# A row-sum kernel whose first block is loaded by four strided DMAs instead of one

## The chip, the cores and the metric

The kernel runs on one core of a Trainium2 chip. The metric is device time in microseconds, from one execution; the median of three runs of the kernel before is 160.64 us (160.61 to 160.81). A profiled execution of the same program gives the time inside: its span runs from the first to the last instruction that the profiler records, and the rest of the execution lies around that span.

## The reference

The input x has the shape 32 x 512 x 1024 in float32, that is 16384 rows of 1024 numbers, 67.1 MB. Each row is summed and the sum multiplied by 0.5; the output is 32 x 512 in float32.

```
def reference(x, multiplier):
    return (np.sum(x, axis=-1) * multiplier).astype(np.float32)
```

## The kernel before

The 16384 rows are spread over the 128 partitions of the on-chip memory (SBUF), 128 rows for each. They are worked through in eight blocks of B = 16 rows for each partition, so that a block is 128 partitions x 16 rows x 4 KB = 8 MB, 64 KB for each partition. In the first seven blocks, a partition's 112 rows lie one after another in the input (`x_rows`, line 43), so that the 64 KB of one partition and block are contiguous there, and neighbouring partitions lie 448 KB apart. The last block (`x_last`, line 44) is the last 2048 rows of the input.

All loads are issued by SyncE, through the helper `load` (lines 73 to 79): one DMA from the input into a buffer, a semaphore of its own that the DMA raises by 16 when all of it has landed, and, from the fourth block on, a wait until VectorE has finished with the buffer (`bufs` = 3 buffers, line 51, used in turn). The DMA queue of SyncE is served by 16 DMA engines that each take a share of a transfer's partitions.

The first three loads wait for nothing. The function `start_loads_at_entry` (lines 184 to 208) moves such leading loads into the program's entry block, ahead of SyncE's part of the barrier with which all engines begin; it takes every load up to the first that has a wait.

In the loop over blocks (lines 104 to 134), VectorE waits for the block's landing (line 114), sums all rows of it in one instruction (`reduce_sum`, lines 115 to 120) and scales the sums into `res` (line 122). In the seventh block VectorE takes eight of the rows and ScalarE the other eight, with one activation each that scales and sums (`act_row`, line 82).

The last block (lines 136 to 174) comes in five pieces of falling size, 10 rows, 4 rows, 1 row with a part of the last row, and the two other parts of that row, so that little is left to sum when the last piece lands. VectorE sums with `dve_sum` (line 92), ScalarE with `act_row`. The outputs of the first seven blocks are stored early (line 151), those of the last one at the end (line 177), and SyncE waits for both.

The change touches the first pass of the loop, where b is 0: its load and the value that VectorE waits for.

Of the kernel before, what the change touches and what calls it, by code (L numbers as in the profile page):

```python
# [9 lines left out]
def kernel(  # L10
# [13 lines left out]
    nc = tc.nc  # L24
# [4 lines left out]
    P = nc.NUM_PARTITIONS  # L29
# [9 lines left out]
    B = 16  # L39
# [3 lines left out]
    x_rows = x_flat[0 : P * own, :].rearrange("(p c) d -> p c d", p=P)  # L43
# [7 lines left out]
    bufs = 3  # L51
# [4 lines left out]
    at = 368  # L56
    end = sbuf("end", P, at + D - cuts[1])

    def sem(name):
        return nc.alloc_semaphore(name=name)  # L60
# [5 lines left out]
    def marks(i, engine):  # L66

        s = dve_done if engine == "dve" else act_done
        i.then_inc(s, 1)
        counts[engine] += 1  # L70
        return counts[engine]

    def load(name, dst, src, free=None):
        landed = sem(name)
        i = nc.sync.dma_start(out=dst, in_=src)  # L75
        if free is not None:
            i.wait_op(dve_done, free, "sem-ge")
        i.then_inc(landed, 16)
        return landed

    def act_row(t, r, col):
        return nc.scalar.activation(  # L82
            out=t[:, r, :],
            in_=t[:, r, :],
            func=mybir.ActivationFunctionType.Copy,
            scale=mul,
            accum_out=res[:, col : col + 1],
        )
# [14 lines left out]
    freed = []  # L103
    for b in range(n_blocks - 1):
        c0 = b * B
        t = buf[b % bufs]
        landed = load(
            f"landed{b}",
            t,
            x_rows[:, c0 : c0 + B, :],  # L110
            freed[b - bufs] if b >= bufs else None,
        )
        h = B if b < n_blocks - 2 else B // 2
        nc.vector.wait_ge(landed, 16)
        done = marks(
            nc.vector.reduce_sum(  # L116
                out=sums[:, c0 : c0 + h], in_=t[:, 0:h, :], axis=mybir.AxisListType.X
            ),
            "dve",
        )  # L120
        freed.append(done)
        scaled = nc.vector.tensor_single_scalar(  # L122
            out=res[:, c0 : c0 + h],
            in_=sums[:, c0 : c0 + h],
            scalar=mul,
            op=mybir.AluOpType.mult,
        )
        scaled.wait_op(dve_done, done, "sem-ge")
        early_dve = marks(scaled, "dve")
        if h < B:  # L130
            nc.scalar.wait_ge(landed, 16)
            for r in range(h, B):
                i = act_row(t, r, c0 + r)
            early_act = marks(i, "act")

    c0 = (n_blocks - 1) * B
    t = buf[(n_blocks - 1) % bufs]
# [4 lines left out]
    landed = [  # L142
        load(f"landed_p{k}", flat[:, lo:hi], flat_last[:, lo:hi])
        for k, (lo, hi) in enumerate(zip(bounds[:-1], bounds[1:]))
    ]
# [11 lines left out]
    for k, (lo, hi) in enumerate(((0, 10), (10, 14), (14, 15))):  # L157
        on = [r for r in range(lo, hi) if r in on_act]
        nc.scalar.wait_ge(landed[k], 16)
        for r in on:  # L160
            i = act_row(t, r, c0 + r)
        late_act = marks(i, "act") if k == len(landed) - 1 else None
        on = [r for r in range(lo, hi) if r not in on_act]
        nc.vector.wait_ge(landed[k], 16)
        for r in on:
            dve_sum(t[:, r, :], res[:, c0 + r : c0 + r + 1], mul)
# [79 lines left out]
```

## Time and profile before

| quantity | value |
|---|---|
| median of 3 runs | 160.64 us (160.61 to 160.81) |
| time of the profiled execution | 160.62 us |
| its span | 159.3 us |
| VectorE busy | 119.9 us, 75% |
| ScalarE busy | 16.3 us, 10% |
| share of the 16 DMA engines that the queue filled | 98.1% |
| read from HBM, mean rate over the span | 67.11 MB, 422 GB/s |
| first reduction of VectorE starts | 21.76 us |
| from a load's issue to its landing, median of 7 | 40.8 us |

In the profile, DVE is VectorE, ACT is ScalarE, POOL is GpSimd and SP is SyncE; SPq is SyncE's sequencer, which issues the DMAs. L116 is line 116 of the kernel. In a timeline, each row has a start and a length in microseconds, engine, line, operation, what is written and read, and how often; square brackets show for how long the engine stood idle before it, and what ended that. In a table of windows, each row has the window and its length, the busy time of the engines with the number of their instructions, the granted clock of TensorE (1.00 here, where it does no work), the share of the DMA engines' time and the rate in GB/s; a DMA packet counts, with all its time and bytes, in the window where it starts. In a chain of waits, each row has a start, a length and what the time went to.

### The profile page before, as it was taken

How to read it: one execution, taken by the hardware profiler on the slowest of the kernel's cores; microseconds unless marked ns; L12 is line 12 of the kernel's file. 1: busy time of each engine (PE TensorE's matmuls, PEld its weight loads, DVE VectorE, ACT ScalarE, POOL GpSimd, SP SyncE). 2: the span in 40 equal slices, each digit the busy share in tenths (PEclk: the TensorE clock that was granted, in tenths of full speed). 3: DMA queues.
4: the chain of work that ended last, by engine and by line, in shares of the span. 5: the costliest groups of instructions: out<-in, count | busy, mean ns of one | idle time of the engine just before them, and what ended most of it. 6: DMA issues, size and time to landing. Idle time of an engine off the chain costs nothing.

```text
span 159.3 us, 123 instructions
## 1 busy us (share of the span) xinstructions
DVE 119.9 (75%) x38; ACT 16.3 (10%) x29; POOL 0.2 (0%) x4
## 2 busy tenths in 40 slices
DVE  0000059998699968999599995999959999598376
ACT  3000000000000000000000000000000000397384
POOL 0000000000000000000000000000000000000000
DMA  7996996997998989969969969969989699799994
GB/s 263 527 527 263 527 527 263 527 477 313 527 411 378 527 346 444 527 280 510 527 263 527 527 263 527 494 296 527 428 362 527 296 494 527 329 432 391 415 404 151
DMA packets 2016, 67.18 MB, mean 422 GB/s; under 512 B 480, under 2 KB 736, under 8 KB 864
## 3 DMA queue, kind: packets, MB, share of 16 engines
q1 hardware_dynamic: 2016, 67.18, 98.1%
HBM read 67.11 MB, written 0.07 MB: 422 GB/s over the span
## 4 chain that ended last, share of the span: by engine, by line
DMA 75%; DVE 24%; SPq 0%; issue 0%
DMA xb<-in_x_dram 75%; DVE sums L116 22%; DVE xb L92 1%; DVE end L92 0%; SPq L75 0%; DVE res L122 0%; DVE res L92 0%
## 5 line engine op out<-in xcount | busy, mean ns | idle before, releaser
L116 DVE TENSOR_REDUCE sums<-xb 128x16 f32<-128x16384 f32 (+1 forms) x7 | 112.0, 16001 | 33.3 <-DMA xb<-in_x_dram 33.3
L82 ACT ACTIVATE xb<-xb 128x1024 f32<-128x1024 f32 x14 | 14.6, 1044 | 139.1 <-DMA xb<-in_x_dram 139.1
L92 DVE CUSTOM_DVE_ANT_0 xb<-xb 128x512 f32<-128x512 f32 (+1 forms) x10 | 5.9, 654 | 4.4 <-DMA xb<-in_x_dram 4.4
L82 ACT ACTIVATION_READ_ACCUMULATOR xb<-xb 128x1 f32 x14 | 2.6, 186 | 0.0
L82 ACT ACT_TABLE_LOAD x1 | 1.3, 1283 | 2.4 <-PEq L26 2.4
L122 DVE TENSOR_SCALAR res<-sums 128x16 f32<-128x16 f32 (+1 forms) x7 | 1.2, 174 | 0.2
L92 DVE DVE_READ_ACCUMULATOR2_ANT res<- 128x1 f32 x10 | 0.8, 82 | 0.0
L92 DVE CUSTOM_DVE_ANT_0 end<-end 128x176 f32<-128x176 f32 (+1 forms) x2 | 0.7, 326 | 0.0
L92 DVE DVE_READ_ACCUMULATOR2_ANT end<- 128x1 f32 x2 | 0.2, 84 | 0.0
L227 POOL MEMSET const-bfloat16-1.0<- 128x1 bf16 x1 | 0.1, 101 | 0.0
L227 POOL MEMSET const-uint8-127<- 128x1 uint8 x1 | 0.1, 101 | 0.0
L227 POOL MEMSET const-float32-0.0<- 128x1 f32 x1 | 0.1, 98 | 0.2 <-issue 0.2
L227 POOL MEMSET const-float32-1.0<- 128x1 f32 x1 | 0.1, 98 | 0.0
## 6 DMA issues: line engine op xcount, KB each, us to landing
xb<-in_x_dram SPq DMA_DIRECT2D x1, 5120.0 KB, 33.6
xb<-in_x_dram SPq DMA_DIRECT2D x1, 2048.0 KB, 38.1
xb<-in_x_dram SPq DMA_DIRECT2D x1, 704.0 KB, 39.3
end<-in_x_dram SPq DMA_DIRECT2D x1, 176.0 KB, 39.3
end<-in_x_dram SPq DMA_DIRECT2D x1, 144.0 KB, 39.2
xb<-in_x_dram SPq DMA_DIRECT2D x7, 40.8
out_dram<-res SPq DMA_DIRECT2D x1, 56.0 KB, 10.8
out_dram<-res SPq DMA_DIRECT2D x1, 8.0 KB, 1.4
```

Source lines behind the costliest of these rows:

```text
L82: return nc.scalar.activation(out=t[:, r, :], in_=t[:, r, :], func=mybir.ActivationFunctionType.Copy, scale=mul, accum_out=res[:, col : co ...
L92: return nc.vector.tensor_tensor_reduce(out=row[:, 0:mid], in0=row[:, 0:mid], in1=row[:, mid:], scale=scale, scalar=0.0, op0=ADD, op1=ADD, ...
L116: nc.vector.reduce_sum(out=sums[:, c0 : c0 + h], in_=t[:, 0:h, :], axis=mybir.AxisListType.X),
L122: scaled = nc.vector.tensor_single_scalar(out=res[:, c0 : c0 + h], in_=sums[:, c0 : c0 + h], scalar=mul, op=mybir.AluOpType.mult,)
L227: nc = _bacc.Bacc("TRN2", target_bir_lowering=False, num_devices=1)
```

## The change

The first block is loaded by four DMAs instead of one. The first takes partitions 0, 8, 16, ... (16 of them), the second 4, 12, 20, ... (16), the third 2, 6, 10, ... (32) and the fourth the odd ones (64). Together they name each of the 128 partitions once. They are issued one after another by SyncE, wait for nothing, and raise one semaphore, by 16 each; VectorE waits for 64 in the first block and for 16 in the others as before. The four are leading loads like the two that follow them, so that `start_loads_at_entry` now moves six loads to the entry block. The intended property is that each DMA engine moves the same partitions as before, in another order.

```diff
+    def load_first(name, dst, src):
+
+        landed = sem(name)
+        for at, step in ((0, 8), (4, 8), (2, 4), (1, 2)):
+            i = nc.sync.dma_start(out=dst[at:P:step], in_=src[at:P:step])
+            i.then_inc(landed, 16)
+        return landed, 64
...
     for b in range(n_blocks - 1):
         c0 = b * B
         t = buf[b % bufs]
-        landed = load(
-            f"landed{b}",
-            t,
-            x_rows[:, c0 : c0 + B, :],
-            freed[b - bufs] if b >= bufs else None,
-        )
+        full = 16
+        if b == 0:
+            landed, full = load_first("landed0", t, x_rows[:, 0:B, :])
+        else:
+            landed = load(
+                f"landed{b}",
+                t,
+                x_rows[:, c0 : c0 + B, :],
+                freed[b - bufs] if b >= bufs else None,
+            )
         h = B if b < n_blocks - 2 else B // 2
-        nc.vector.wait_ge(landed, 16)
+        nc.vector.wait_ge(landed, full)
```

## The prediction

> **What bounds the kernel now.** I read the page's busy time, slices, queue and chain first, then the chain of waits in order of time, the timelines of SyncE and VectorE, and last the windows around the start.
>
> From the page:
>
> ```profile
> span 159.3 us, 123 instructions
> DVE 119.9 (75%) x38; ACT 16.3 (10%) x29; POOL 0.2 (0%) x4
> ...
> q1 hardware_dynamic: 2016, 67.18, 98.1%
> HBM read 67.11 MB, written 0.07 MB: 422 GB/s over the span
> ```
>
> The 16 DMA engines are busy 98.1% of the span; VectorE, the next, 75%. The timeline of VectorE shows what it waits for:
>
> ```profile
> 21.76 17.22 DVE L116 TENSOR_REDUCE sums<-xb 128x16 f32<-128x16384 f32 x1 [21.76 <-DMA xb<-in_x_dram]
> 39.02 0.17 DVE L122 TENSOR_SCALAR res<-sums 128x16 f32<-128x16 f32 x1
> 41.09 17.22 DVE L116 TENSOR_REDUCE sums<-xb 128x16 f32<-128x16384 f32 x1 [1.90 <-DMA xb<-in_x_dram]
> 58.34 0.17 DVE L122 TENSOR_SCALAR res<-sums 128x16 f32<-128x16 f32 x1
> 60.44 17.22 DVE L116 TENSOR_REDUCE sums<-xb 128x16 f32<-128x16384 f32 x1 [1.92 <-DMA xb<-in_x_dram]
> ```
>
> Blocks arrive 19.33 and 19.35 us apart, VectorE needs 17.22 + 0.17 us, and it idles 1.9 us per block for the next landing. So the transfers set the pace, and a delay of block 0 moves every later landing by as much: the queue never runs dry. (Block 3's load is issued at 39.0, when VectorE frees its buffer, while block 2 lands only at 60.4; if block 0 lands later by d, both move by d.) The chain's end shows that the tail hangs on landings too:
>
> ```profile
> 116.77 38.09 DMA xb<-in_x_dram
> 154.87 0.02 issue
> 154.89 0.69 DVE xb L92
> ```
>
> The start, in windows. The last figure is GB/s counted where a transfer packet starts; a packet here is one partition's row of 64 KB, so 655 in a window of 0.1 us is one packet:
>
> ```profile
> 0.90:1.00 0.10, 0.00 (x0) 0.00 (x0) 0.00 (x0) 1.00 0.00 0
> 1.00:1.10 0.10, 0.00 (x0) 0.00 (x0) 0.00 (x0) 1.00 9.62 3277
> 1.10:1.20 0.10, 0.00 (x0) 0.00 (x0) 0.00 (x0) 1.00 5.95 1966
> 1.20:1.30 0.10, 0.00 (x0) 0.00 (x0) 0.00 (x0) 1.00 7.57 2621
> 1.30:1.40 0.10, 0.00 (x0) 0.00 (x0) 0.00 (x0) 1.00 1.94 655
> 1.40:1.50 0.10, 0.00 (x0) 0.00 (x0) 0.00 (x0) 1.00 3.61 1311
> 1.50:1.60 0.10, 0.00 (x0) 0.00 (x0) 0.00 (x0) 1.00 1.86 655
> 1.60:4.00 2.40, 0.00 (x0) 1.28 (x1) 0.00 (x0) 1.00 0.00 0
> 4.00:4.10 0.10, 0.00 (x0) 0.00 (x0) 0.00 (x0) 1.00 6.05 2621
> ...
> 4.40:4.50 0.10, 0.00 (x0) 0.00 (x0) 0.00 (x0) 1.00 6.04 2621
> ```
>
> 5, 3, 4, 1, 2 and 1 packets start between 1.0 and 1.6 us: 16, one for each engine, spread over half a microsecond. The second packets start from 4.0 to 4.5, a spread of 0.4 to 0.5 us that nothing later removes. From there each engine moves a row in 19.35 / 8 = 2.42 us (27.1 GB/s; 433 GB/s for sixteen).
>
> **The change part by part.** The sum is made against the profiled execution: 160.62 us, of which 159.3 are the span and 1.3 lie around it; it stands 0.02 below the median of 160.64.
>
> *Bytes and rows: nothing.* Each engine still has eight rows of block 0 (1 + 1 + 2 + 4), if each transfer spreads evenly: 8 x 2.42 = 19.35 us of work. Queue, tile and later transfers are unchanged.
>
> *Three more issues on SyncE: nothing at the end.* The first three issues take 0.38, 0.42 and 0.43 us, the third ending at 1.32. Three more at 0.43 (0.46 with the gap) bring the sixth to 2.7 us. What stands behind them on SyncE: the loads of blocks 1 and 2, not reached by an engine before 21 us; and the entry barrier, which ScalarE's table load (2.38, 1.28 us long) waits for and which then comes 1.4 us later. ScalarE's first row is at 137.87 and VectorE's first wait ends at 21.76, so that cover is large. The second transfer is issued by 0.85 us; a first packet followed its issue's end by 0.62 us (0.38 to 1.00), so it stands ready at 1.5, before any engine has ended its first row at 4.0. If this cover were gone, each late issue would cost 0.46 us.
>
> *Three more completions, and VectorE's wait for 64 in place of 16: nothing.* The wait still ends with the last landing, and only VectorE's own reduction stands behind it. An interval of 19.35 us with one completion differs from eight rows by less than 0.05 us, so three more cost 0 to 0.15. I take 0, the end that the rows lie at.
>
> *The start's spread: a gain.* The first issue names 16 rows instead of 128, one for each engine, so less stands before the last engine's first row. Most: all second packets start with the earliest, 4.45 - 4.05 = 0.40, or 0.50 by the first starts. Least: 0. A loss is excluded by the ready times above. I take -0.40, since the spread exists in the transfer's first rows alone and one row in eight is what remains of it.
>
> *How fast the rows of the partial transfers go: the term that decides.* Every load of before names all 128 partitions, and no row shows a strided subset. Lower bound: rows go at 2.42, cost 0; a gain beyond that is excluded, as no full block runs faster. Upper bound: two engines share a way into the tile, and their rows take 4.84 instead of 2.42. That is +2.42 for each row so moved: +4.84 for the two 16-partition transfers, one row per engine each, and 6 x 2.42 = +14.5 for the 32- and 64-partition ones. [...] The 64- and 32-partition transfers stand nearest to the 128-row rows: I take 0 for them. The 16-partition ones, one partition in eight, stand farthest: I take +4.84.
>
> [...]
>
> *Sum:* 0 + 0 + 0 - 0.40 + 4.84 + 0 = +4.4 us: span 163.7, time 165.0.
>
> **The rivals.**
>
> 1. *Rows keep 2.42 us, and only the start's spread goes* (the other side). For it: every row of the trace has that pace, and the first starts are visibly spread. Against: those rows are of full transfers alone. Place: block 0's landing, 21.3 to 21.4 instead of 21.7. Price: -0.50 to 0, so 160.1 to 160.6, likeliest 160.25. It decides if the second rows still start by 4.1 us.
> 2. *Sharing costs half as much.* One engine of a sharing pair goes first, the other waits one row, and then the two are out of step and share no more: one row of 2.42 lost instead of two, +2.42 - 0.40: 162.7. For it: starts up to 0.5 us apart; against: the gain's own mechanism brings the starts together.
> 3. *All four transfers run at half rate:* +4.84 + 14.5 - 0.4 = +18.9: 179.6. For it: nothing but that the 32- and 64-partition transfers are unseen as well. Block 0 would land near 40 us.
> 4. *The change doesn't do what it says:* a 16-partition transfer is carried by fewer than 16 engines. With eight engines of two rows each, the same eight twice, they get 4 + 6 = 10 rows instead of 8: +4.84 again; the two sets of eight complementary: 0. Both times are already among the cases above (165.0 and rival 1), and the count of first packets in the windows would tell them apart.
>
> **How the numbers follow.** Forecast, with rival 4's first form: 0.64, in 164.4 to 165.7 (gain 0.5 to nothing, completions 0 to 0.15). Rival 2: 0.17, 162.2 to 164. Rival 1 with rival 4's second form: 0.14. Rival 3: 0.05. About 0.2% (0.32 us) is what a measurement of this kernel can tell from no change. Rival 1 lies on that edge (160.25 against 160.32): 0.08 faster, 0.06 the same. Slower is the rest, 0.86. The range takes in the forecast and rival 2, which leaves out 0.19: 162.2 to 165.8. Its ends are rival 2 with the largest gain, and the forecast with no gain and all completions paid.
>
> **What would show it.** Right: in the windows the first packets all start within some 0.15 us of 1.0 to 1.1; the second ones only near 6.5 (1.05, plus 4.84, plus the 0.6 by which a first row is longer than 2.42 in before), the third near 11.3; from there 2.42 us a row; VectorE's first reduction starts near 26.2 instead of 21.76, and every later interval is 19.35. SyncE's issues end near 2.7 us. Wrong: second packets by 4.1 us mean no sharing (rival 1); a part of them near 4 and a part near 6.5, rival 2; the first reduction near 40 us, rival 3; eight first packets in the place of sixteen, rival 4. The prediction fails most simply if a partial transfer is as wide as a full one.

## The result: 166.0 us, and where 5.3 us came from

The changed kernel takes 166.0 us (median of six runs, 165.87 to 166.21) against 160.72 us for the kernel before (median of six, 160.61 to 160.81): a ratio of 1.033, interval 1.0318 to 1.0345. It is slower, as forecast, and the slow rows stand where they were forecast; but 165.0 with an upper end of 165.8 was too low.

The page of the changed kernel:

```profile
span 164.7 us, 126 instructions
...
DVE 119.8 (73%) x38; ACT 16.3 (10%) x29; POOL 0.2 (0%) x4
...
q1 hardware_dynamic: 2064, 67.18, 97.8%
HBM read 67.11 MB, written 0.07 MB: 408 GB/s over the span
```

The span is 5.4 us longer (164.7 against 159.3) and the engines do the same work in it. The DMA engines still look full, 97.8%. That share is time in which packets were under way, not bytes: the rate over the span fell from 422 to 408 GB/s. There are 48 packets more (2064 against 2016), 16 for each of the three further transfers, and all of them under 512 bytes (528 of that size against 480).

VectorE's timeline:

```profile
27.15 17.22 DVE L128 TENSOR_REDUCE sums<-xb 128x16 f32<-128x16384 f32 x1 [27.15 <-DMA xb<-in_x_dram]
44.40 0.17 DVE L134 TENSOR_SCALAR res<-sums 128x16 f32<-128x16 f32 x1
46.49 17.22 DVE L128 TENSOR_REDUCE sums<-xb 128x16 f32<-128x16384 f32 x1 [1.91 <-DMA xb<-in_x_dram]
63.74 0.17 DVE L134 TENSOR_SCALAR res<-sums 128x16 f32<-128x16 f32 x1
65.84 17.22 DVE L128 TENSOR_REDUCE sums<-xb 128x16 f32<-128x16384 f32 x1 [1.93 <-DMA xb<-in_x_dram]
```

The first block lands 5.39 us later (27.15 against 21.76), the second comes 19.34 us after it and the third 19.35 after that, as before. All of the loss lies in block 0 and nothing later makes up for it. The chain of waits has the start and, near the end, the last stretches of the path:

```profile
0.00 0.60 SPq L85
0.60 0.06 issue
0.66 0.57 SPq L85
...
122.17 38.08 DMA xb<-in_x_dram
160.24 0.02 issue
160.27 0.69 DVE xb L100
```

The last landing before the final sums is at 160.24 instead of 154.87, 5.37 later. At the top is a surprise: the first load issue takes SyncE 0.60 us, where the full load took 0.38. The chain of the kernel before begins with this line:

```profile
0.00 0.38 SPq L75
```

Now block 0 itself, row by row. In the windows the last two figures are the share of the 16 DMA engines' time and the rate, both counted where a packet starts. Rate times length gives the packets (953 GB/s x 1.1 us = 1.05 MB = 16 rows of 64 KB), and since these are 16 packets on 16 engines, share times length is the mean duration of one. The kernel before:

```profile
1.00:1.60 0.60, 0.00 (x0) 0.00 (x0) 0.00 (x0) 1.00 5.09 1748
4.00:4.50 0.50, 0.00 (x0) 0.00 (x0) 0.00 (x0) 1.00 4.84 2097
6.40:6.90 0.50, 0.00 (x0) 0.00 (x0) 0.00 (x0) 1.00 4.84 2097
```

First, second and third row take 3.05 (5.09 x 0.60), 2.42 and 2.42 us. The changed kernel:

```profile
1.30:2.40 1.10, 0.00 (x0) 0.00 (x0) 0.00 (x0) 1.00 4.31 953
2.40:5.80 3.40, 0.00 (x0) 1.12 (x1) 0.00 (x0) 1.00 0.00 0
5.80:7.20 1.40, 0.00 (x0) 0.16 (x1) 0.00 (x0) 1.00 3.54 749
7.20:10.70 3.50, 0.00 (x0) 0.00 (x0) 0.00 (x0) 1.00 0.00 0
10.70:12.10 1.40, 0.00 (x0) 0.00 (x0) 0.00 (x0) 1.00 2.06 749
12.10:13.90 1.80, 0.00 (x0) 0.00 (x0) 0.00 (x0) 1.00 0.00 0
13.90:14.60 0.70, 0.00 (x0) 0.00 (x0) 0.00 (x0) 1.00 3.46 1498
```

Sixteen packets are under way at once from 2.4 us on, so all sixteen engines carry the 16-partition transfers. The rows take 4.74 and 4.96 us in these two, 2.88 in the first row of the 32-partition transfer, and 2.42 from there. Three rows take 12.58 us instead of 7.89: +4.69. The rest is in the start, in windows of 0.1 us (those between hold no packet):

```profile
1.30:1.40 0.10, 0.00 (x0) 0.00 (x0) 0.00 (x0) 1.00 5.95 1311
1.40:1.50 0.10, 0.00 (x0) 0.00 (x0) 0.00 (x0) 1.00 9.23 1966
1.50:1.60 0.10, 0.00 (x0) 0.00 (x0) 0.00 (x0) 1.00 12.42 2621
1.60:1.70 0.10, 0.00 (x0) 0.00 (x0) 0.00 (x0) 1.00 5.77 1311
1.90:2.00 0.10, 0.00 (x0) 0.00 (x0) 0.00 (x0) 1.00 2.95 655
2.00:2.10 0.10, 0.00 (x0) 0.00 (x0) 0.00 (x0) 1.00 5.36 1311
2.10:2.20 0.10, 0.00 (x0) 0.00 (x0) 0.00 (x0) 1.00 2.71 655
2.30:2.40 0.10, 0.00 (x0) 0.00 (x0) 0.00 (x0) 1.00 2.98 655
```

With 655 for one packet, as before, these are 2, 3, 4, 2, 1, 2, 1 and 1 packets. Taken at the middle of its window, the mean first packet starts at 1.694 instead of 1.219 us, +0.48, and the first starts reach to 2.4 instead of 1.6. Some 0.2 of the 5.39 is left. By windows of 0.1 us at the first row of block 1, the last engine is 0.32 us behind the mean instead of 0.18, which accounts for 0.14 of it.

### The profile page after: what moved, and what is told of

Its sections match the earlier page's. It is cut to its first block, busy times and chain, and to the rows that moved or that the text cites. A ratio compares the mean times of both kernels' runs of the same rounds, so it can differ in the third digit from the quotient of the medians.

```text
span 164.7 us, 126 instructions
## 1 busy us (share of the span) xinstructions
DVE 119.8 (73%) x38; ACT 16.3 (10%) x29; POOL 0.2 (0%) x4
## 2 busy tenths in 40 slices
DMA packets 2064, 67.18 MB, mean 408 GB/s; under 512 B 528, under 2 KB 784, under 8 KB 912
## 3 DMA queue, kind: packets, MB, share of 16 engines
q1 hardware_dynamic: 2064, 67.18, 97.8%
## 4 chain that ended last, share of the span: by engine, by line
DMA 75%; DVE 23%; SPq 2%; issue 0%
DMA xb<-in_x_dram 75%; DVE sums L128 21%; SPq L85 1%; DVE xb L100 1%; DVE end L100 0%; DVE res L134 0%; SPq L75 0%; DVE res L100 0%
```

## The experiments

The theory, which the expectations call shared ways, was the author's assumption for the rows of 4.74 and 4.96 us where 2.42 is the pace: in a 16-partition transfer two DMA engines hold each other up on a way into the tile. No trace names a way; what the experiments vary, and can tell, is which sets of partitions have slow rows. Four rivals: any transfer with a partition step is slow; any transfer of few partitions is slow; the sources far apart in HBM (the memory that holds the input) collide; the loss belongs to the idle start. All times stand against runs of the kernel before on the same chip.

### No transfer of 16 partitions

```diff
-        for at, step in ((0, 8), (4, 8), (2, 4), (1, 2)):
+        for at, step in ((0, 4), (2, 4), (1, 2)):
...
-        return landed, 64
+        return landed, 48
```

> Block 0 by three transfers (every fourth partition, every fourth from 2, every second from 1): the two 16-partition transfers are made one of 32. Theory of shared ways (two engines write through one way into the tile, which happens in the 16-partition transfers alone): no row is slowed, so +4.84 goes and only the change of the start stays, which the changed kernel puts at +0.4 to +0.6: 160.9 to 161.3. Rival, any transfer with a partition step is slowed: the loss stays, 163 or more. The first load issue of SyncE is expected at 0.60 us if the partition step lengthens it, at 0.38 if the small number of partitions does.

Measured: 161.16 us against 160.71, ratio 1.0029 (1.0017 to 1.0040). Windows of this kernel around its first and second rows:

```profile
1.30:1.90 0.60, 0.00 (x0) 0.00 (x0) 0.00 (x0) 1.00 5.36 1748
...
4.40:5.10 0.70, 0.00 (x0) 0.70 (x1) 0.00 (x0) 1.00 3.46 1498
```

The second row takes 2.42 us (3.46 x 0.70): with the two 16-partition transfers merged into one of 32, the slow rows are gone, step or no step. What is left is +0.45, all at the start: the first packets come at 1.3 instead of 1.0, after a first issue of 0.54 us, on average 0.26 us later (by windows of 0.1 us), and the first row takes 3.22 us (5.36 x 0.60) instead of 3.05. In the profiled execution (161.18 us) the first reduction starts at 22.31, 0.55 late.

### Two halves, even and odd, and two halves of neighbours

```diff
-        for at, step in ((0, 8), (4, 8), (2, 4), (1, 2)):
+        for at, step in ((0, 2), (1, 2)):
...
-        return landed, 64
+        return landed, 32
```

> Block 0 by two transfers of 64 partitions, the even ones and the odd ones. Shared ways: both reach as much as a full transfer, rows stay at 2.42 us, 160.7 to 161.3 (the start only). Rival, a transfer that names fewer than 128 partitions is slower by their number: some 180 (half rate for 19.35 us of rows).

Measured: 161.01 us, ratio 1.0019 (1.0010 to 1.0028).

```diff
-        for at, step in ((0, 8), (4, 8), (2, 4), (1, 2)):
-            i = nc.sync.dma_start(out=dst[at:P:step], in_=src[at:P:step])
+        for lo, hi in ((0, 64), (64, 128)):
+            i = nc.sync.dma_start(out=dst[lo:hi], in_=src[lo:hi])
...
-        return landed, 64
+        return landed, 32
```

> Block 0 by two transfers of 64 partitions, 0 to 63 and 64 to 127, without a step. [...] Rivals (the step, or the sources 3.5 MB apart in HBM, or one row for an engine in a transfer is what slows): none of these is there, 160.7 to 161.2. The first issue tells whether SyncE needs 0.60 us without a step.

Measured: 182.35 us, ratio 1.135 (1.133 to 1.137). This pair decides against number and step: both kernels have two transfers of 64 partitions, and the stepped one is the fast one. Which 64 they are makes 21 us of difference. The +21.6 is more than the +19.35 that a doubling of block 0's eight rows would cost. The first issue took 0.55 us without a step.

### The four transfers on block 1

```diff
-        if b == 0:
-            landed, full = load_first("landed0", t, x_rows[:, 0:B, :])
+        if b == 1:
+            landed, full = load_first("landed1", t, x_rows[:, c0 : c0 + B, :])
```

> Block 0 by one transfer as before, block 1 by the four transfers. The engines are busy when these come, so the start is that of before and only the slowed rows are left: +4.84, 165.5. If a part of the changed kernel's +5.3 that I put to the start belongs to the four transfers themselves, 166.0; if the slowing needs the idle start (all engines beginning at once), 160.7.

Measured: 165.97 us, ratio 1.0333 (1.0318 to 1.0349). That is neither 165.5 nor 160.7 but the 166.0 of the expectation's second case: on engines that are already busy, the four transfers cost the whole 5.3 us. Its windows around the three rows in question, when the engines are all busy:

```profile
20.90:21.50 0.60, 0.00 (x0) 0.00 (x0) 0.00 (x0) 1.00 7.69 1748
...
25.30:26.40 1.10, 1.10 (x1) 0.00 (x0) 0.00 (x0) 1.00 4.46 953
...
30.10:31.30 1.20, 1.20 (x1) 0.00 (x0) 0.00 (x0) 1.00 2.38 874
...
33.20:33.90 0.70, 0.70 (x1) 0.00 (x0) 0.00 (x0) 1.00 3.46 1498
```

The rows take 4.61, 4.91, 2.86 and then 2.42 us: three rows take 12.38 instead of 7.26, +5.12 and not +4.84. So the price is higher than a doubling of two rows, because the third row, already of the 32-partition transfer, takes 0.44 us more than 2.42. Its first and its last packet:

```profile
30.10:30.20 0.10, 0.10 (x1) 0.00 (x0) 0.00 (x0) 1.00 1.96 655
...
31.20:31.30 0.10, 0.10 (x1) 0.00 (x0) 0.00 (x0) 1.00 1.63 655
```

Each of these windows has one packet, on one engine of sixteen, so it takes 16 x 1.96 x 0.10 = 3.14 us in the first window and 2.61 in the last. The engine that comes to this row first takes longer than the one that comes last, as it would if it were still held up by engines that are at their second slow row. (That is argued; the traces do not show what holds a packet up.) In the changed kernel the same three rows cost 4.69, as the engines start there one after the other and a first row is 0.6 longer anyway. With the late start, 0.48, that comes to nearly the same sum as here, 5.17 against 5.12, and nothing in the theory asks for that.

The first block starts here as in the kernel before, its first packets from 1.0 us on. Yet its reduction starts later, though its last rows end by 21.5 us:

```profile
22.23 17.22 DVE L128 TENSOR_REDUCE sums<-xb 128x16 f32<-128x16384 f32 x1 [22.23 <-DMA xb<-in_x_dram]
```

In the kernel before, the last rows end by 21.4 and the reduction starts at 21.76. So the completion comes some 0.4 us later in this run, where the rows behind it take 4.61 us and more; why was not tried. It is no part of the 5.3: the next rows start from 20.9 us on and do not wait for it.

### Other sources, same destinations

```diff
-        for at, step in ((0, 8), (4, 8), (2, 4), (1, 2)):
-            i = nc.sync.dma_start(out=dst[at:P:step], in_=src[at:P:step])
+        for at, step, lo, hi in ((0, 8, 0, 16), (4, 8, 16, 32), (2, 4, 32, 64), (1, 2, 64, 128)):
+            i = nc.sync.dma_start(out=dst[at:P:step], in_=src[lo:hi])
```

> The four transfers write the same partitions as in the changed kernel, but read neighbouring rows of the input (0 to 15, 16 to 31, 32 to 63, 64 to 127), so block 0's sums come out under other partitions: the output's order in those 16 columns is not the reference's. Theory of shared ways into the tile: nothing changes, 166.0 (165.8 to 166.2). Rival, the sources 3.5 MB apart in HBM are what slows: 160.9 to 161.3.

Measured: 166.63 us, ratio 1.0366 (1.0352 to 1.0380): above the range of the theory, and far from the rival's. The loss stays when the source rows of the 16-partition transfers lie 448 KB apart instead of 3.5 MB, so spread sources are not its cause. Its first two rows, by windows:

```profile
1.30:3.10 1.80, 0.00 (x0) 0.00 (x0) 0.00 (x0) 1.00 2.88 583
...
6.20:7.70 1.50, 0.00 (x0) 0.00 (x0) 0.00 (x0) 1.00 3.28 699
```

The kernel with eight transfers of 16 neighbours (the first of the next section) reads the very same addresses in its first two rows, and writes them to 16 neighbouring partitions:

```profile
1.00:2.30 1.30, 0.00 (x0) 0.00 (x0) 0.00 (x0) 1.00 6.48 807
...
8.40:10.90 2.50, 0.00 (x0) 0.00 (x0) 0.00 (x0) 1.00 3.67 419
```

With the same sources, a row takes 5.18 and 4.92 us here, and 8.42 and 9.18 there. So it is the partitions written that decide.

Another 0.6 us came on top of the changed kernel's time. The first packets start anywhere from 1.3 to 3.1 us, on average no later than in the changed kernel (1.68 against 1.69, by windows of 0.1 us), but the first row takes 5.18 us instead of 4.74. I did not find out why.

### More slow rows: eight transfers, by neighbours and by step, and four of 32

```diff
-        for at, step in ((0, 8), (4, 8), (2, 4), (1, 2)):
-            i = nc.sync.dma_start(out=dst[at:P:step], in_=src[at:P:step])
+        for lo in range(0, P, 16):
+            i = nc.sync.dma_start(out=dst[lo : lo + 16], in_=src[lo : lo + 16])
...
-        return landed, 64
+        return landed, 128
```

> Block 0 by eight transfers of 16 neighbouring partitions, without a step. [...] Rival, a transfer of 16 partitions runs at half rate whichever they are: 8 x 2.5 more, 181.

Measured: 214.6 us, ratio 1.335 (1.333 to 1.338), far from the rival's 181.

```diff
-        for at, step in ((0, 8), (4, 8), (2, 4), (1, 2)):
+        for at, step in [(at, 8) for at in range(8)]:
...
-        return landed, 64
+        return landed, 128
```

> Block 0 by eight transfers of every eighth partition, from 0, 1, 2 and so on. [...] Doubling alone (4.84) would give 180.4.

Measured: 182.23 us, ratio 1.134 (1.132 to 1.135), 1.8 above the 180.4 of a doubling, which has eight rows of 2.42 us more (19.4) and 0.3 for the late start. Its rows take 5.07 us on average from the second to the eighth (its window is below), as those of the two neighbouring halves do.

```diff
-        for at, step in ((0, 8), (4, 8), (2, 4), (1, 2)):
-            i = nc.sync.dma_start(out=dst[at:P:step], in_=src[at:P:step])
+        for lo in range(0, P, 32):
+            i = nc.sync.dma_start(out=dst[lo : lo + 32], in_=src[lo : lo + 32])
```

> Block 0 by four transfers of 32 neighbouring partitions, without a step. [...] SyncE's first issue: 0.39 us if it is the partition step that lengthens it (16 neighbouring partitions took 0.389), 0.55 if it is the number of partitions between 16 and 128 (64 neighbouring ones took 0.552).

Measured: 181.92 us, ratio 1.132 (1.129 to 1.134), 0.4 below the two neighbouring halves (182.35). The first issue took 0.39 us.

One window of each kernel, over its second to eighth row (seven rows on sixteen engines, 7.34 MB). First the two neighbouring halves from above:

```profile
5.90:41.40 35.50, 0.00 (x0) 0.00 (x0) 0.00 (x0) 1.00 1.00 207
```

Eight transfers of every eighth partition:

```profile
6.00:41.50 35.50, 0.00 (x0) 1.28 (x1) 0.00 (x0) 1.00 1.00 207
```

Four transfers of 32 neighbours:

```profile
5.50:41.10 35.60, 0.00 (x0) 0.00 (x0) 0.00 (x0) 1.00 1.00 206
```

Eight transfers of 16 neighbours:

```profile
8.40:72.40 64.00, 0.00 (x0) 0.00 (x0) 0.00 (x0) 1.00 1.00 115
```

Every engine has a packet under way all the time (share 1.00), yet they pass 206 to 207 GB/s in the first three kernels and 115 in the last; a full block passes 433. A row takes 5.07 us (35.5 / 7) or 9.14 us (64.0 / 7) instead of 2.42. That a transfer of 16 partitions runs at half rate whichever they are would have made 181 of the last one, not 214.6. No run has a transfer of 16 partitions whose rows take 2.42 us, so the runs do not show whether the number 16 costs something by itself. With 32 and with 64 partitions there are rows of 2.42 us and rows of 5.1, so there the number does not decide.

By the sets of partitions, the rows of these kernels and those before take, from the second on: 2.42 us with every second partition (3.02 x 0.80 in the window from 4.3 to 5.1 us of the even and odd halves) and with every fourth (3.46 x 0.70, above); 4.9 to 5.1 us with every eighth; 5.1 us with 64 and with 32 neighbours; 9.1 us with 16 neighbours. What the slow sets have in common that the others have not, no trace shows.

### As many full transfers, by rows

```diff
-        for at, step in ((0, 8), (4, 8), (2, 4), (1, 2)):
-            i = nc.sync.dma_start(out=dst[at:P:step], in_=src[at:P:step])
+        for lo, hi in ((0, 2), (2, 4), (4, 8), (8, 16)):
+            i = nc.sync.dma_start(out=dst[:, lo:hi, :], in_=src[:, lo:hi, :])
```

> Block 0 by four transfers of all 128 partitions, with 2, 2, 4 and 8 of the 16 rows, on one semaphore: as many transfers, of the same sizes, as in the changed kernel, but none of them partial. If transfers that name fewer than 128 partitions are what lengthens SyncE's issue to 0.55 to 0.60 us and delays the first packet to 1.3 to 1.4: first issue 0.38, first packets at 1.0, and the time that of before plus what 32 smaller packets for each engine cost in the place of 8, some 0.2 us: 160.7 to 160.95. If the number of transfers on the empty queue or the shared semaphore does it: first packets at 1.3 or later and 161.1 or more.

Measured: 160.86 us against 160.75, ratio 1.0008 (0.9999 to 1.0017). Its chain begins, and its VectorE timeline begins, with these lines:

```profile
0.00 0.38 SPq L85
```

```profile
21.90 17.22 DVE L128 TENSOR_REDUCE sums<-xb 128x16 f32<-128x16384 f32 x1 [21.90 <-DMA xb<-in_x_dram]
```

Four transfers, three more completions and one semaphore for all of them cost 0.1 us here (0 to 0.3 by the interval), with the smaller packets included. So neither the number of transfers nor the wait for 64 is in the 5.3. The first issue is back at 0.38 us and first packets start between 1.0 and 1.1.

### The four in reverse

```diff
-        for at, step in ((0, 8), (4, 8), (2, 4), (1, 2)):
+        for at, step in ((1, 2), (2, 4), (4, 8), (0, 8)):
```

> The four transfers of the changed kernel in reverse order: the odd partitions first, the two 16-partition transfers last. If the late start (+0.30 measured where block 0 begins with a 64-partition transfer of step 2) and the shared rows on busy engines (+5.26 measured in block 1) add, 160.7 + 0.30 + 5.26 = 166.3. If the order of the four decides what the sharing costs, 165.5 or less. Its first packets are expected at 1.33 us.

Measured: 166.74 us, ratio 1.0376 (1.0359 to 1.0394), its runs from 166.26 to 167.0. The late start and the full price of the slow rows stand side by side here, and their sum is 0.4 below the median; the runs differ more than those of the other kernels, and that remainder is unexplained. The first packets come from 1.3 us on, as expected. The order does not save anything.

### What lengthens the first issue

SyncE's first issue, and the window in which the first packets come:

| first transfer | first issue, us | first packets from |
|---|---|---|
| 128 partitions (before) | 0.38 | 1.0 |
| 128, two rows each | 0.38 | 1.0 |
| 16 neighbours | 0.39 | 1.0 |
| 32 neighbours | 0.39 | 1.0 |
| 64 neighbours | 0.55 | 1.3 |
| 64, step 2 (even ones; odd ones in the reversed kernel) | 0.55; 0.58 | 1.3 |
| 32, step 4 | 0.54 | 1.3 |
| 16, step 8 (changed kernel and two others) | 0.57 to 0.60 | 1.3 |

Each longer issue goes with a first packet some 0.3 us later. A step of partitions lengthens it in every case; few partitions alone do not. But 64 neighbours are long without a step, so a step is not the whole rule, and what it is stays open.

## Why the prediction was right and wrong

*Bytes and rows: right.* Each engine has eight rows of block 0, 2.42 us each once the first three are past, and later blocks keep their interval (19.34 and 19.35).

*Issues on SyncE: hidden as said, but mis-sized.* The four took 0.57 to 0.60 us instead of the 0.43 read from full transfers, so that the sixth issue ended at 3.61 us instead of 2.7, and ScalarE's table load came at 4.67, 2.3 us later and not 1.4. The second to sixth are covered, as argued. The first is not: nothing hides the time until the first packet, and I had not priced it as a term.

*Completions and the wait for 64: right*, by the run with four full transfers (0.1 us).

*The start's spread: the step that failed.* It said -0.40, "a loss is excluded". Measured is a loss: first packets start 0.48 us later on average, and lie further apart (1.3 to 2.4 instead of 1.0 to 1.6). Two things were wrong in it. The spread does not come from a transfer's naming eight rows for each engine: with one row each it grew. And the ready times with which I excluded a loss were those of the second transfer, worked out from the issue of a full one. They say nothing of the first packet, which waits for the very issue that the change replaces. A row for that issue's duration was missing, and it should have been bounded from above. On their own such starts cost 0.45 us (three transfers) and 0.30 us (even and odd halves).

*The partial transfers' rows: rightly placed, but for a wrong reason.* +4.84 was forecast for the two 16-partition transfers and 0 for the others, as these stand nearer to 128 partitions. The number of partitions does not decide: halves of neighbours run at about half the rate (207 GB/s against 433), and 32 partitions of step 4 at 2.42 us a row, as fast as all 128. That two engines share a way, the case behind +4.84, no run shows; the runs showed rows of 4.74 and 4.96 us in these two transfers. The size was met with some luck. The rows cost +4.69 in the changed kernel, but as +1.69, +2.54 and +0.46 in the first three rows, where +2.42, +2.42 and 0 were forecast. On busy engines they cost +5.12, so that a doubling of two rows was not the upper bound that the prediction made of it.

*The sum.* 4.44 was forecast; 0.88 more from the start, 0.15 less from the rows and some 0.2 for the last engine make 5.37. That is what the profiled executions show (166.0 less 160.62). The range's upper end had no loss at the start in it, and so missed. Its ends also do not follow from the terms: with these, rival 2 with the largest gain is 162.5, where 162.2 stands, and the forecast without a gain and with all completions 165.6, where 165.8 stands.

*The rivals.* No sharing: excluded, second rows start after 5.8 us. Half the price by falling out of step: the second row, 4.96 us, is no shorter than the first, 4.74, so no such gain is seen. All four at half rate: excluded, 2.42 us from the fourth row on. Fewer engines: excluded, 16 packets at once. Which engine holds which partition the traces do not tell, so that the intended property, that each engine moves the partitions it moved before, was not tested. If it holds, it does not keep the rate: on every eighth partition a row took 4.7 to 5.0 us.

## What to carry to other kernels

What a load that names part of the partitions costs depends on which they are: even and odd halves cost 0.3 us, at the start (161.0 us), lower and upper halves 21.6 (182.4). Why these sets differ was not shown. The division that cost least here goes along the transfer's rows and keeps all 128 partitions (160.9). Where a change replaces the first instruction of the critical path, that instruction's own duration is a term of the sum, and a neighbour of another shape does not bound it (0.60 us where full loads took 0.38 to 0.43); and a DMA share near 100% says that packets were under way, not that bytes flowed (1.00 at 115 GB/s with 16 neighbours, 1.00 at 433 in a full block).

## What was not expected of the hardware

The slow rows are not slower by whole factors. The 5.07 us of the two neighbouring halves is 2.1 times the 2.42 of a full block, the 9.14 us of 16 neighbours 3.8 times. Why the one is more than a doubling and the other less than two was not tried.

The first row of 32 partitions, after the two of 16, is slow too: 2.86 us on average instead of 2.42 in the kernel with the four transfers on block 1, from 3.14 for the engine that starts it first to 2.61 for the last. So in that kernel the price of slow rows reaches into the transfer behind them, most for the engine that is ahead.
